# Matmuls that read hi first and lo last in every group, and rotations and rows of scales asked for later

## The chip, the cores and the metric

The kernel runs on one core of one Trainium2 chip. The metric is device time in microseconds (us) of one execution, lower is better. The kernel before takes 2664.11 us, the median of three runs (2663.95 to 2665.12).

## The reference

Two layers of an encoder on 256 tokens of width 2048, in float32. Cut to what matters:

```python
for l in range(DEPTH):                                  # DEPTH = 2
    u = rmsnorm(x, norm_mix[l])
    c_q, c_kv, k_pe, q_na, k_na, v_na, gate_a, gate_b = split(u @ w_in[l])
    q  = rmsnorm(c_q,  norm_qa[l])  @ w_uq[l]           # 8 heads of 128 + 64 (rotary)
    kv = rmsnorm(c_kv, norm_kva[l]) @ w_ukv[l]          # 8 heads of 128 + 128
    y_a = mla_attention(q_nope, rope(q_pe), k_nope, rope(k_pe), v) @ w_o_mla[l]
    y_b = neighbourhood_attention(q_na, k_na, v_na, rpb[l]) @ w_o_na[l]
    x = x + (sigmoid(gate_a) * y_a + sigmoid(gate_b) * y_b) @ w_out[l]
    h = rmsnorm(x, norm_mlp[l]) @ w_ff1[l]              # 2048 -> 8192
    x = x + square(relu(h)) @ w_ff2[l]                  # 8192 -> 2048
return rmsnorm(x, norm_final)
```

Nearly all of the arithmetic is products of 256 rows with weight matrices of 2048 or more rows and columns, some 490 MB of them read once.

## The kernel before, in words

**Split operands.** Every float32 operand of a product is split in two: `hi` is the value rounded to the matmul's input type `F32R`, `lo` is the rest. A product then is three matmuls into one PSUM bank: activation hi times weight hi, activation hi times weight lo, activation lo times weight hi. The product lo times lo is left out. Activations are split once. Weights are split as they arrive: a DMA on the SP queue brings `raw`, ScalarE (ACT) casts `hi <- raw` (line 177 or 201), and VectorE (DVE) subtracts `lo <- raw - hi` (line 178 or 202). `raw` has 3 buffers; `hi` and `lo` have 4 each in the first half of a layer and 3 each in the second half (`strips`), where a buffer holds 2048 columns instead of 1024.

**Forms of a product.**
- `gemm_a` (weights stream, activations stand; lines 232 to 234 through `mm_a`): two banks, one for each 128 tokens. A group is two k-blocks of 128 rows: for each of the two banks 2 x 3 matmuls of 512 columns, then one `tick()`.
- `gemm_b` (activations stream, weights stand; lines 223 and 224 through `mm_b`): four banks. A pair is one matmul of 512 columns with `wh`, which covers activation hi and lo at once, and one of 256 columns with `wl`. A group is 4 x 2 pairs with a `tick()` after every second pair.
- `gemm_s` (line 414 through `mm3`): 1024 columns of the weights at a time with up to eight banks. A step `j` takes 256 rows of the weights. A step that is not in `pairs` has 8 products of 3 matmuls (24). A step in `pairs` is a Strassen-like one with 7 products (21 matmuls): DVE forms four sums of the four weight blocks (lines 446, 449, 450) into `sums`, which ACT and DVE split in hi and lo as well. The first three products (1, 2, 3) read `raw`, the last four (5, 7, 6, 4) read `sums`. There are 110 such steps, one for each instruction of line 446. At the first step in `pairs`, `drain()` asks for all pending work at once.

**What else runs.** Smaller work (heads of the attention, norms, transposes, rotations) is written as generators on a list `pending`. `tick()` counts a clock and advances one generator whose time has come; `yield n` and `start(gen, n)` mean "not before n more ticks". So ticks, not times, place this work among the matmuls. `rows_of` turns a column of scales into a row (DVE builds `diag`, TensorE multiplies with ones on line 283). `rope` is a rotation: a TensorE product with a permutation (line 517), three DVE operations and a split. `turned` transposes a merged tile on TensorE (line 484) after DVE has written it (lines 782, 783). `evac` functions empty the banks when a product is done.

**Order.** The kernel is built with `tile.TileContext(nc, schedule_with_timeline_sim=True)`: the order in the source is a priority, and a planner with its own estimates of durations writes each engine's queue before the program runs. An engine takes its queue in that order.

Of the kernel before, what the change touches and what calls it, by code (L numbers as in the profile page):

```python
# [39 lines left out]
P = 128  # L40
S = 256
# [10 lines left out]
NC = D // P  # L52
# [23 lines left out]
def trunk(ctx: ExitStack, tc: tile.TileContext, x, w_in, w_uq, w_ukv, rpb, w_o_mla, w_o_na,  # L76
# [80 lines left out]
    def have(acts, k):  # L157

        while acts[k] is None:
            advance(min(range(len(pending)), key=lambda i: pending[i][0]))  # L160
        return acts[k]
# [59 lines left out]
    def mm_b(ps, wh, wl, a, first, last):  # L221

        nc.tensor.matmul(ps, wh, a, start=first, stop=False)  # L223
        nc.tensor.matmul(ps[:, :S], wl, a[:, :S], start=False, stop=last)  # L224

    def mm_a(ps, a, t, wh, wl, first, last):

        if isinstance(a, list):
            ah, al = a[0][t], a[1][t]
        else:  # L230
            ah, al = a[:, t * P:(t + 1) * P], a[:, S + t * P:S + (t + 1) * P]
        nc.tensor.matmul(ps, ah, wh, start=first, stop=False)  # L232
        nc.tensor.matmul(ps, ah, wl, start=False, stop=False)  # L233
        nc.tensor.matmul(ps, al, wh, start=False, stop=last)  # L234

    def mm_3(ps, ah, al, bh, bl, first, last):
# [11 lines left out]
    def gemm_a(w, c0, acts, evac):  # L248

        nk = len(acts)  # L250
        ps = [bank() for _ in range(2)]
        for k0, wh, wl in weights(w, nk, c0, 512):
            for t in range(2):
                for k in range(k0, k0 + 2):
                    mm_a(ps[t], have(acts, k), t, wh[:, k - k0], wl[:, k - k0], k == 0, k == nk - 1)
                tick()
        for t in range(2):
            evac(t, ps[t])

    def gemm_b(w, c0, acts, evac, before=None, ahead=None):  # L260

        nk = len(acts)
        ps = [bank() for _ in range(4)]
        for k0, wh, wl in weights(w, nk, c0, 512, before):
            for m in range(4):
                ms = slice(m * P, (m + 1) * P)
                for k in range(2):
                    mm_b(ps[m], wh[:, k, ms], wl[:, k, ms], have(acts, k0 + k), k0 + k == 0, k0 + k == nk - 1)
                tick()
        if ahead:  # L270
            ahead()
        for m in range(4):
            evac(m, ps[m])

    def rows_of(col):

        dg = [keep.tile([P, P], F32, tag="diag", name="diag", bufs=4) for _ in range(2)]
        for t in range(2):
            nc.vector.tensor_scalar_mul(dg[t], ident, col[:, t:t + 1])
        yield 5  # L280
        pb = abank()
        for t in range(2):
            nc.tensor.matmul(pb[:, t * P:(t + 1) * P], ones, dg[t], start=True, stop=True)
        row = keep.tile([P, S], F32, tag="rrow", name="rrow", bufs=4)
        nc.vector.tensor_copy(row, pb[:, :S])
        return row
# [113 lines left out]
    def gemm_s(w, c0, get, order, pairs, evac):  # L400
# [7 lines left out]

        def mm3(i, ah, al, wh, wl):
            if i not in b:  # L410
                b[i], count[i] = bank(), 0
            for x, y in ((ah, wh), (ah, wl), (al, wh)):
                count[i] += 1
                nc.tensor.matmul(b[i], x, y, start=count[i] == 1, stop=count[i] == total[i])  # L414

# [8 lines left out]
        for j in order:  # L424
# [3 lines left out]
            if j not in pairs:  # L428
                ws = cut(raw)
                for k in range(2):  # L430
                    left, right = ws[2 * k:2 * k + 2]
                    ah, al = get(j)
                    for i, t, side in ((2, 0, right), (3, 0, left), (4, 1, right), (8, 1, left)):
                        mm3(i, ah[2 * k + t], al[2 * k + t], *side)
                        if t:
                            tick()
                continue
# [15 lines left out]
            (a11, _, a12, a22, s1, s2, s3, s4), (l11, _, l12, l22, r1, r2, r3, r4) = get(j)  # L453
            mm3(1, a11, l11, *w11)
            mm3(2, a12, l12, *w21)
            tick()
            mm3(3, s4, r4, *w22)
            mm3(5, s1, r1, *w1)
            tick()
            mm3(7, s3, r3, *w3)  # L460
            mm3(6, s2, r2, *w2)
            tick()
            mm3(4, a22, l22, *w4)
        r11, r22, r12, r21 = (wide() for _ in range(4))
# [182 lines left out]
    for l in range(DEPTH):  # L647
# [15 lines left out]
        for g in range(2):  # L663
# [5 lines left out]
            for k0, wh, wl in weights(wi, NC, C_VN + g * 512, 512):  # L669
                for t in range(2):  # L670
                    for k in range(k0, k0 + 2):
                        mm_a(ps[t], xg[k], t, wh[:, k - k0], wl[:, k - k0], k == 0, k == NC - 1)
                    tick()
                    tick()
            vt = [values(ps[t], mix.col, t) for t in range(2)]
# [26 lines left out]
        nc.vector.tensor_tensor(t, t, mix.row, op=ALU.mult)  # L702
        start(rope(t, key_pe(ke)), 4)

# [28 lines left out]
        for g in range(4):  # L733
# [7 lines left out]
            nc.vector.tensor_tensor(t, t, nq.row, op=ALU.mult)  # L741
            start(rope(t, query_pe(qr)), 3)
            for m in range(2):
# [207 lines left out]
```

## Time and profile before

| what | us |
|---|---|
| median of three runs | 2664.11 |
| the profiled execution | 2664.57 |
| its span, first to last instruction | 2662.8 |
| TensorE matmul (PE) busy | 2616.6 (98%) |
| TensorE weight load (PEld) busy | 2181.1 (82%) |
| VectorE (DVE) busy | 2121.3 (80%) |
| ScalarE (ACT) busy | 1461.4 (55%) |

The mean granted TensorE clock is 0.999. DMA engines are busy 55% of the span with the weights' queue. A matmul's duration in the profile runs over the start of the next one, since they are pipelined: what a matmul takes from the others is the distance from its start to the next start. A row of the view of waits reads: who waited, for whom, microseconds in total, times, longest.

### The profile page before, as it was taken

The numbers are of one execution on the slowest core, as the hardware profiler recorded it, in microseconds if no ns is written. First come the engines' busy times: TensorE is split into PE (matmuls) and PEld (weight loads), VectorE is DVE, ScalarE is ACT, GpSimd is POOL, SyncE is SP. The second block draws the span as 40 slices with busy tenths as digits, with TensorE's granted clock in tenths as the row PEclk, the third lists the DMA queues.
The fourth block names the chain that finished last, engine by engine and source line by source line (L and its number), as shares of the span: only waits on it lengthen the run. The fifth ranks groups of instructions, "written<-read, shape, count | busy, mean of one in ns | idle before, by whom it ended". The sixth has DMA issues, their size and how long they took to land.

```text
span 2662.8 us, 31999 instructions
## 1 busy us (share of the span) xinstructions
PE 2616.6 (98%) x12498; PEld 2181.1 (82%) x12498; DVE 2121.3 (80%) x2496; ACT 1461.4 (55%) x1719; POOL 94.8 (4%) x117
## 2 busy tenths in 40 slices
PE   8999999999999999999999999999999999999998
PEld 7888888877888888888888888888788888888886
DVE  6678789688888787888667788896988888878885
ACT  6555456446555545546555555564565555455553
POOL 0100000000000010000001100000000000100000
PEclk9999999999999999999999999999999999999999
DMA  7555554455567485675555555544555765756744
GB/s 245 176 159 196 195 201 147 158 174 188 192 201 237 163 239 197 197 236 177 189 185 179 165 191 190 203 141 152 182 202 172 219 206 196 236 199 194 253 168 144
DMA packets 175256, 508.95 MB, mean 191 GB/s; under 512 B 13696, under 2 KB 18176, under 8 KB 175104
## 3 DMA queue, kind: packets, MB, share of 16 engines
q1 hardware_dynamic: 166192, 490.08, 55.2%
q0 software_dynamic: 8768, 16.78, 3.2%
q8 instruction: 98, 1.61, 0.2%
q14 instruction: 54, 0.44, 0.0%
q10 hardware_dynamic: 144, 0.04, 0.0%
HBM read 492.18 MB, written 2.10 MB: 186 GB/s over the span
## 4 chain that ended last, share of the span: by engine, by line
PE 68%; issue 21%; DVE 6%; ACT 3%; POOL 1%; DMA 0%; POOLq 0%; DVEq 0%; ACTq 0%; SPq 0%
PE bank L414 40%; PE bank L223 8%; PE bank L224 4%; PE bank L232 4%; PE bank L233 4%; PE bank L234 4%; DVE lo L178 3%; ACT hi L177 2%; PE bank L383 1%; PE bank L239 1%; PE bank L238 1%; PE bank L237 1%; DVE wide L465 1%; DVE sums L446 1%; POOL xt L862 1%
## 5 line engine op out<-in xcount | busy, mean ns | idle before, releaser
L414 PE MATMUL bank<-hi,pair 128*128 128x512 f32 x5156 | 1604.8, 391 | 9.8 <-ACT hi L177 9.1
L414 PEld LDWEIGHTS bank<-hi,pair 128*128 128x128 f32 x5156 | 965.6, 188 | 221.9 <-ACT hi L177 23.5
L414 PE MATMUL bank<-lo,pair 128*128 128x512 f32 x2578 | 1006.6, 391 | 7.7 <-DVE lo L178 7.7
L177 ACT CAST hi<-raw 128x2048 fp32r<-128x2048 f32 (+3 forms) x416 | 632.4, 1534 | 433.8 <-PE bank L414 302.4
L178 DVE TENSOR_TENSOR lo<-raw,hi 128x2048 fp32r<-128x2048 f32 (+3 forms) x416 | 752.0, 1817 | 117.6 <-ACT hi L177 115.9
L414 PEld LDWEIGHTS bank<-lo,pair 128*128 128x128 f32 x2578 | 483.9, 188 | 114.2 <-DVE lo L178 14.9
L178 DVE TENSOR_TENSOR lo<-sums,hi 128x2048 fp32r<-128x2048 f32 (+1 forms) x134 | 255.9, 1909 | 161.5 <-ACT hi L177 161.4
L202 DVE TENSOR_TENSOR lo<-raw,hi 128x1024 fp32r<-128x1024 f32 (+1 forms) x224 | 270.2, 1212 | 141.1 <-ACT hi L201 140.8
L177 ACT CAST hi<-sums 128x2048 fp32r<-128x2048 f32 (+1 forms) x134 | 214.8, 1603 | 286.1 <-DVE sums L450 185.0
L223 PE MATMUL bank<-pair,hi 128*128 128x512 f32 x960 | 344.5, 402 | 3.7 <-ACT hi L201 3.7
L201 ACT CAST hi<-raw 128x1024 fp32r<-128x1024 f32 (+1 forms) x224 | 229.9, 1035 | 205.2 <-PE bank L234 96.1
L224 PE MATMUL bank<-pair,lo 128*128 128x256 f32 x960 | 264.5, 281 | 0.0
L232 PE MATMUL bank<-hi,pair 128*128 128x512 f32 (+1 forms) x576 | 218.9, 381 | 0.0
L233 PE MATMUL bank<-lo,pair 128*128 128x512 f32 (+1 forms) x576 | 218.6, 380 | 0.0
L234 PE MATMUL bank<-hi,pair 128*128 128x512 f32 (+1 forms) x576 | 217.2, 378 | 0.0
L465 DVE TENSOR_TENSOR wide<-wide,bank 128x512 f32<-128x512 f32 x336 | 215.3, 678 | 0.1
L223 PEld LDWEIGHTS bank<-pair,hi 128*128 128x128 f32 x960 | 180.5, 189 | 42.2 <-ACT hi L201 4.5
L224 PEld LDWEIGHTS bank<-pair,lo 128*128 128x128 f32 x960 | 181.7, 189 | 2.3
L446 DVE TENSOR_TENSOR sums<-raw 128x1024 f32<-128x1024 f32 x110 | 134.1, 1219 | 21.9 <-DMA raw<-in_w_ff 14.5
L234 PEld LDWEIGHTS bank<-hi,pair 128*128 128x128 f32 x576 | 108.3, 188 | 19.9
L232 PEld LDWEIGHTS bank<-hi,pair 128*128 128x128 f32 x576 | 108.3, 188 | 20.0
L233 PEld LDWEIGHTS bank<-lo,pair 128*128 128x128 f32 x576 | 108.4, 188 | 18.9
(123 smaller groups left out, 1557.0 us busy)
## 6 DMA issues: line engine op xcount, KB each, us to landing
raw<-in_w_ff SPq DMA_DIRECT2D x256, 1024.0 KB, 5.3
raw<-in_w_in SPq DMA_DIRECT2D x124, 1024.0 KB, 5.1
raw<-in_w_out SPq DMA_DIRECT2D x32, 1024.0 KB, 5.3
raw<-in_w_o_na SPq DMA_DIRECT2D x16, 1024.0 KB, 5.1
raw<-in_w_o_mla SPq DMA_DIRECT2D x16, 1024.0 KB, 5.0
xt<-wide POOLq DMA_DIRECT2D x48, 256.0 KB, 7.3
raw<-in_w_ukv SPq DMA_DIRECT2D x8, 1024.0 KB, 5.5
raw<-in_w_uq SPq DMA_DIRECT2D x8, 768.0 KB, 4.6
```

Source lines behind the costliest of these rows:

```text
L177: nc.scalar.copy(hi, src)
L178: nc.vector.tensor_tensor(lo, src, hi.bitcast(F32), op=ALU.subtract)
L201: nc.scalar.copy(hi, src)
L202: nc.vector.tensor_tensor(lo, src, hi.bitcast(F32), op=ALU.subtract)
L223: nc.tensor.matmul(ps, wh, a, start=first, stop=False)
L224: nc.tensor.matmul(ps[:, :S], wl, a[:, :S], start=False, stop=last)
L232: nc.tensor.matmul(ps, ah, wh, start=first, stop=False)
L233: nc.tensor.matmul(ps, ah, wl, start=False, stop=False)
L234: nc.tensor.matmul(ps, al, wh, start=False, stop=last)
L414: nc.tensor.matmul(b[i], x, y, start=count[i] == 1, stop=count[i] == total[i])
L446: nc.vector.tensor_tensor(ts[0].rearrange("p (a n) -> p a n", a=2), raw[:, :512].rearrange("p (a n) -> p a n", a=1).to_broadcast([P, 2, 512]),
L465: add = lambda o, a, c: nc.vector.tensor_tensor(o, a, c, op=ALU.add)
```

## The change

Within each group of `gemm_a`, `gemm_b` and `gemm_s` all matmuls that read `hi` of the weights are asked for first and those that read `lo` last. In `gemm_s` a step's 7 or 8 products are now handed to `products`, which issues two matmuls of each with `wh`, with a tick after every second product, and then one of each with `wl`. `gemm_a` becomes `group_a`, with a third tick after the lo matmuls; the values' product of the neighbourhood attention, which had four ticks a group, uses it too with one more tick (four again). The products with `mm_b` and `mm_a` in the loops over `w_uq`, `w_ukv` and the key rotation's columns stay as they are. `rows_of` yields 8 ticks instead of 5; the key rotation is started 8 ticks after its input instead of 4, the query rotations 7 instead of 3. The number, shapes and operands of all matmuls are the same.

```diff
+    def group_a(ps, acts, k0, nk, wh, wl):
+        for t in range(2):
+            for k in range(2):
+                for i, a in enumerate(sides(have(acts, k0 + k), t)):
+                    nc.tensor.matmul(ps[t], a, wh[:, k], start=k0 + k + i == 0, stop=False)
+            tick()
+        for t in range(2):
+            for k in range(2):
+                nc.tensor.matmul(ps[t], sides(have(acts, k0 + k), t)[0], wl[:, k], start=False, stop=k0 + k == nk - 1)
+        tick()
...
 gemm_a:
-            for t in range(2):
-                for k in range(k0, k0 + 2):
-                    mm_a(ps[t], have(acts, k), t, wh[:, k - k0], wl[:, k - k0], k == 0, k == nk - 1)
-                tick()
+            group_a(ps, acts, k0, nk, wh, wl)
 gemm_b:
             for m in range(4):
                 for k in range(2):
-                    mm_b(ps[m], wh[:, k, ms], wl[:, k, ms], have(acts, k0 + k), ...)
+                    nc.tensor.matmul(ps[m], wh[:, k, m * P:(m + 1) * P], have(acts, k0 + k), ...)
                 tick()
+            for m in range(4):
+                for k in range(2):
+                    nc.tensor.matmul(ps[m][:, :S], wl[:, k, m * P:(m + 1) * P], have(acts, k0 + k)[:, :S], ...)
 rows_of:
-        yield 5
+        yield 8
 gemm_s:
+        def products(*todo):
+            for n, (i, ah, al, wh, wl) in enumerate(todo):
+                mm(i, ah, wh)
+                mm(i, al, wh)
+                if n % 2:
+                    tick()
+            for i, ah, al, wh, wl in todo:
+                mm(i, ah, wl)
...
-            mm3(1, a11, l11, *w11)
-            mm3(2, a12, l12, *w21)
-            tick()
-            mm3(3, s4, r4, *w22)
-            mm3(5, s1, r1, *w1)
-            tick()
-            mm3(7, s3, r3, *w3)
-            mm3(6, s2, r2, *w2)
-            tick()
-            mm3(4, a22, l22, *w4)
+            products((1, a11, l11, *w11), (2, a12, l12, *w21), (3, s4, r4, *w22), (5, s1, r1, *w1),
+                     (7, s3, r3, *w3), (6, s2, r2, *w2), (4, a22, l22, *w4))
...
-        start(rope(t, key_pe(ke)), 4)
+        start(rope(t, key_pe(ke)), 8)
...
-            start(rope(t, query_pe(qr)), 3)
+            start(rope(t, query_pe(qr)), 7)
```

More of the change, by code (lines that the diff above doesn't have):

```diff
@@ L224, in mm_b, with sides @@
         nc.tensor.matmul(ps[:, :S], wl, a[:, :S], start=False, stop=last)
+    def sides(a, t):
+        if isinstance(a, list):
+            return a[0][t], a[1][t]
+        return a[:, t * P:(t + 1) * P], a[:, S + t * P:S + (t + 1) * P]
     def mm_a(ps, a, t, wh, wl, first, last):
[L228 to L231, printed above, removed]
+        ah, al = sides(a, t)
         nc.tensor.matmul(ps, ah, wh, start=first, stop=False)
@@ L265, in gemm_b @@
             for m in range(4):
-                ms = slice(m * P, (m + 1) * P)
                 for k in range(2):
-                    mm_b(ps[m], wh[:, k, ms], wl[:, k, ms], have(acts, k0 + k), k0 + k == 0, k0 + k == nk - 1)
+                    nc.tensor.matmul(ps[m], wh[:, k, m * P:(m + 1) * P], have(acts, k0 + k), start=k0 + k == 0, stop=False)
                 tick()
+            for m in range(4):
+                for k in range(2):
+                    nc.tensor.matmul(ps[m][:, :S], wl[:, k, m * P:(m + 1) * P], have(acts, k0 + k)[:, :S],
+                                     start=False, stop=k0 + k == nk - 1)
         if ahead:
@@ L407, in gemm_s, with mm @@
                 total[i] += 3 if j in pairs else 6
-        def mm3(i, ah, al, wh, wl):
+        def mm(i, x, y):
             if i not in b:
                 b[i], count[i] = bank(), 0
-            for x, y in ((ah, wh), (ah, wl), (al, wh)):
-                count[i] += 1
-                nc.tensor.matmul(b[i], x, y, start=count[i] == 1, stop=count[i] == total[i])
+            count[i] += 1
+            nc.tensor.matmul(b[i], x, y, start=count[i] == 1, stop=count[i] == total[i])
+        def products(*todo):
[6 more added lines that the diff above has]
+                mm(i, ah, wl)
         def cut(src):
@@ L429, in gemm_s @@
                 ws = cut(raw)
[L430 to L435, printed above, removed]
-                            tick()
+                ah, al = get(j)
+                products(*((i, ah[2 * k + t], al[2 * k + t], *ws[2 * k + side])
+                           for k in range(2) for i, t, side in ((2, 0, 1), (3, 0, 0), (4, 1, 1), (8, 1, 0))))
                 continue
@@ L453, in gemm_s @@
             (a11, _, a12, a22, s1, s2, s3, s4), (l11, _, l12, l22, r1, r2, r3, r4) = get(j)
-            mm3(1, a11, l11, *w11)
-            mm3(2, a12, l12, *w21)
-            tick()
-            mm3(3, s4, r4, *w22)
-            mm3(5, s1, r1, *w1)
-            tick()
-            mm3(7, s3, r3, *w3)
-            mm3(6, s2, r2, *w2)
-            tick()
-            mm3(4, a22, l22, *w4)
+            products((1, a11, l11, *w11), (2, a12, l12, *w21), (3, s4, r4, *w22), (5, s1, r1, *w1),
+                     (7, s3, r3, *w3), (6, s2, r2, *w2), (4, a22, l22, *w4))
         r11, r22, r12, r21 = (wide() for _ in range(4))
@@ L669, in trunk @@
             for k0, wh, wl in weights(wi, NC, C_VN + g * 512, 512):
[L670 to L674, printed above, removed]
+                group_a(ps, xg, k0, NC, wh, wl)
+                tick()
             vt = [values(ps[t], mix.col, t) for t in range(2)]
```

## The prediction, made before the change was run

> **What bounds the kernel now.** I read the page's busy times first, then the view of waits, then the timeline at a few of those waits, then groups by shape.
>
> ```profile
> span 2662.8 us, 31999 instructions
> PE 2616.6 (98%) x12498; PEld 2181.1 (82%) x12498; DVE 2121.3 (80%) x2496; ACT 1461.4 (55%) x1719; POOL 94.8 (4%) x117
> ```
>
> TensorE is the bound: the same 12498 matmuls run after the change, so only the time that PE stands still, and the distance between two matmuls, can change. The view of waits says what it stands still for.
>
> ```profile
> PEld bank L414 <- ACT hi L177: 23.5, 34, 1.0
> PEld bank L414 <- DVE lo L178: 14.9, 22, 1.8
> PE bank L414 <- ACT hi L177: 9.1, 24, 0.5
> PE bank L414 <- DVE lo L178: 7.7, 11, 1.4
> PE bank L484 <- DMA xt<-in_x: 4.9, 1, 4.9
> PE bank L517 <- DVE small L741: 4.1, 4, 1.5
> PE bank L223 <- ACT hi L201: 3.7, 2, 2.5
> PE bank L484 <- DVE wide L783: 3.3, 4, 1.2
> PE bank L283 <- DVE diag L279: 1.0, 2, 0.5
> ACT hi L177 <- PE bank L414: 397.2, 231, 6.0
> DVE lo L178 <- ACT hi L177: 277.3, 209, 3.5
> ACT hi L177 <- DVE sums L450: 185.0, 41, 7.1
> ```
>
> PE's own rows hold 33.8 us, of which the waits for x and for line 201 are mostly the start. The last three rows are the loop behind the waits of line 414: ACT waits 231 times until PE has let go of a `hi` buffer, and DVE's `lo` follows ACT. How much one wait costs is seen in the timeline at 562 us:
>
> ```profile
> 562.50 0.19 PEld L414 LDWEIGHTS bank<-lo,pair 128*128 128x128 f32 x1 [1.85 <-DVE lo L178]
> 562.50 0.50 PE L414 MATMUL bank<-lo,pair 128*128 128x512 f32 x1 [1.43 <-DVE lo L178]
> 562.84 0.39 PE L414 MATMUL bank<-hi,pair 128*128 128x512 f32 x1
> 563.07 0.40 PE L414 MATMUL bank<-lo,pair 128*128 128x512 f32 x1
> ```
>
> Undisturbed matmuls start 0.23 us apart (562.84, 563.07), though each is shown as 0.39 long. So an idle time in PE's rows leaves out 0.39 - 0.23 = 0.16 us, and the first matmul after a wait takes 0.34 instead of 0.23 (562.50 to 562.84), 0.11 more. A wait in these rows costs its idle time and 0.27 us.
>
> **The change, part by part.**
>
> *Waits for lo (`gemm_s`).* Today the second matmul of a step reads lo, 0.23 us after the first. After, it comes behind all 14 or 16 hi matmuls, 3.2 to 3.7 us in. The longest wait for lo is 1.4 us on PE, 1.8 on PEld, so all go, if DVE is not slower. What is there: 7.7 + 11 x 0.27 = 10.7 us. By PEld's rows, whose loads start 0.23 apart and take 0.19, it would be at most 14.9 - 22 x 0.04 = 14.0. What hides lo afterwards are the hi matmuls; were hi late too, the gain would be nil. I take 10.7.
>
> *Waits for hi (`gemm_s`).* The order moves no hi matmul behind anything new, but its buffer is free sooner: today the last matmul of a step reads hi, after the change 7 or 8 lo matmuls stand behind the last one that does, 1.6 to 1.8 us. Whether the late cast was waiting for that buffer is seen at two places:
>
> ```profile
> 736.90 1.92 ACT L177 CAST hi<-raw 128x2048 fp32r<-128x2048 f32 x1 [2.70 <-PE bank L414]
> 739.23 1.48 ACT L177 CAST hi<-raw 128x1536 fp32r<-128x1536 f32 x1
> 740.77 0.50 PE L414 MATMUL bank<-hi,pair 128*128 128x512 f32 x1 [0.28 <-ACT hi L177]
> 569.23 3.29 ACT L177 CAST hi<-raw 128x2048 fp32r<-128x2048 f32 x2
> 569.66 1.07 PE L414 MATMUL bank<-hi,pair 128*128 128x512 f32 x4
> 571.19 0.97 PE L414 MATMUL bank<-hi,pair 128*128 128x512 f32 x3 [0.46 <-ACT hi L177]
> ```
>
> At 736.90 ACT had idled 2.70 us for the buffer, and the next cast, 1.48 long, came 0.28 late: 1.6 us earlier there removes it. At 569.23 two casts follow each other with no idle time, so ACT was late for another reason, and an earlier buffer alone doesn't help. There is a second help: at 569.66 PE had run ahead with four hi matmuls, because the planner thought lo late; with lo asked for last it has less reason to. Present: 9.1 + 24 x 0.27 = 15.6 us (at most 23.5 - 34 x 0.04 = 22.1 by PEld). Ends: all gone, or none. I take two thirds, 10.4, nearer to the first row, because 231 waits of ACT for the buffer speak for it.
>
> *Which stages.* The losses sit where DVE is fullest, around w_out and the first ff1, and at the start of each ff2:
>
> ```profile
> 545.00:625.00 80.00, 75.52 (x332) 60.57 (x333) 69.69 (x76) 42.57 (x47) 0.00 (x0) 1.00 0.57 185
> 733.00:763.00 30.00, 29.21 (x129) 23.14 (x127) 24.31 (x28) 19.02 (x19) 0.00 (x0) 1.00 0.51 172
> ```
>
> PE (first number after the length) lacks 4.5 of 80 us in the first, twice in the program, and 0.8 of 30 in the second, eight times. DVE (third) is busy 87% and 81%: there is room to catch up, not much.
>
> *Order in `gemm_b`.* 12 calls of 8 groups, each of 8 matmuls of 512 and 8 of 256 columns.
>
> ```profile
> 1503.22 0.40 PE L223 MATMUL bank<-pair,hi 128*128 128x512 f32 x1
> 1503.46 0.28 PE L224 MATMUL bank<-pair,lo 128*128 128x256 f32 x1
> ```
>
> The third such pair after it ends where the next 512 columns start; and near the start of the program the planner put some in a row:
>
> ```profile
> 1504.28 0.40 PE L223 MATMUL bank<-pair,hi 128*128 128x512 f32 x1
> ```
>
> ```profile
> 23.02 1.09 PE L223 MATMUL bank<-pair,hi 128*128 128x512 f32 x4
> 23.95 0.28 PE L224 MATMUL bank<-pair,lo 128*128 128x256 f32 x1
> 24.30 0.40 PE L224 MATMUL bank<-pair,lo 128*128 128x256 f32 x2
> ```
>
> In turn, three pairs take 1504.28 - 1503.22 = 1.06 us, 0.353 a pair. In a row, 512 columns follow each other at (1.09 - 0.40) / 3 = 0.230, 256 columns at 0.40 - 0.28 = 0.12. A group becomes 7 x 0.230 + 0.24 + 7 x 0.12 + 0.117 = 2.81 instead of 2.82: 0.01 to 0.02 less, for 96 groups 1 to 2 us; with the rounding of these rows between 0 and 5. I take 2. The Trainium skill, "TensorE: Matmul & The Clock Gate", section Back-to-back issue gap, gives the distance as columns over the clock and a small constant, 216 ns for 512 columns and 109 for 256 as an estimate from that page, whatever stands next to what; by that the order would be worth exactly nothing, and the sum 2 us less. The rows (230 and 120, and 240 in turn) disagree mildly, and they decide.
>
> *Rotations of the queries.* `rope` is asked for 4 ticks later; a tick there is two pairs, 0.7 us, so 2.8 us more cover than today, against waits of at most 1.5 us. Present: 4.1 + 4 x 0.16 = 4.7 us. If the planner had already put it where it thought DVE ready, it may move less than 2.8; ends 0 and 4.7, I take 4.5, since the four waits exceed their cover by less than what is added. The heads that read the rotated queries are queued after 12 ticks, so nothing waits in turn.
>
> *Rows of scales.* The two waits of line 283 (1.0 us) come after the `drain()` of the first gate product, which asks at once, whatever `yield` says: nil, at most 1.3.
>
> *Key rotation.* Eight ticks after its start that same drain comes, so the rotation's DVE work (three operations of 0.42 and two splits) now meets the first sums:
>
> ```profile
> 231.07 0.42 DVE L521 TENSOR_TENSOR small<-small 128x256 f32<-128x256 f32 x1
> ```
>
> Five of these are 2.1 us in front of the sums in each layer: between 0 and 4.2 us, I take 1 lost, since lo has its new slack there.
>
> *Merges before w_out.* `gemm_a` ticks three times a group instead of two, so `turned`, four ticks after a merge, is asked for after 16 matmuls instead of 24, 1.8 us sooner, while the bank it waits for is finished later (below). Line 484 already waits 3.3 + 4 x 0.16 = 3.9 us. Six merges could lose up to 1.8 each, 10.8; the planner may also put it right, 0. I take half of what is there, 2.0 lost.
>
> *Queues.* SP's loads wait for `raw`, which lo frees; lo comes no later, so they move sooner or not at all. POOL's loads of the bias keep their ticks.
>
> ```profile
> SPq L426 <- DVE lo L178: 1385.5, 271, 13.3
> ```
>
> *End.* The last `gemm_a` finishes its first bank 2 matmuls before its end instead of 6; 0.2 us later for the final norm.
>
> Sum against the profiled execution: 2664.6 - 10.7 - 10.4 - 2 - 4.5 + 1 + 2 + 0.2 = 2640.2. That execution is 0.5 above the median of the runs, so 2639.7, say **2640**.
>
> **The rivals.**
>
> *B, hi stays late.* Lo's waits go, hi's all stay: 2639.7 + 10.4 = 2650. For it: 569.23 above. Against it: the 231 waits for the buffer.
>
> *C, the change does not do what it says.* The planner already puts hi first wherever it expects lo late (569.66: four hi in a row, which the source never has more than two of). If it sees the same lateness in the new order, the waits of line 414 stay and only the rotations gain: 2664.1 - 4.5 + 3.2 = 2663. Against it: waits for lo are there today, so its expectations are off by more than nothing.
>
> *D, slower: hi of the sums is needed sooner.* In each of the 110 Strassen steps the sums' hi is read after 6 matmuls instead of 9, 0.69 us sooner, and DVE makes them:
>
> ```profile
> L177 ACT CAST hi<-sums 128x2048 fp32r<-128x2048 f32 x86 | 164.4, 1912 | 214.8 <-DVE sums L450 185.0 <-PE bank L414 29.1
> L178 DVE TENSOR_TENSOR lo<-sums,hi 128x2048 fp32r<-128x2048 f32 x86 | 197.1, 2292 | 130.3 <-ACT hi L177 130.2
> L178 DVE TENSOR_TENSOR lo<-raw,hi 128x1536 fp32r<-128x1536 f32 x86 | 150.7, 1752 | 15.0 <-ACT hi L177 14.9
> L446 DVE TENSOR_TENSOR sums<-raw 128x1024 f32<-128x1024 f32 x110 | 134.1, 1219 | 21.9 <-DMA raw<-in_w_ff 14.5 <-DMA raw<-in_w_in 6.8
> L450 DVE TENSOR_TENSOR sums<-raw,sums 128x512 f32<-128x512 f32 x110 | 75.4, 686 | 1.4
> ```
>
> A step costs DVE 1.22 + 2 x 0.69 + 1.75 + 2.29 = 6.6 us (line 449 as 450), against 21 x 0.23 = 4.8 on PE. If a step loses 0.69 + 0.11 = 0.80, 31 steps eat up the gain of 24.4; with half of the 110, 2640 + 44 = 2684. For it: ACT waits 185 us for line 450. Against it: PE waited for any cast only 24 times, most casts lie well ahead, and the sums' buffer is free 1.6 us sooner as well.
>
> *E, slower: banks finish together.* All four banks of a `gemm_b` now end within 8 x 0.12 us: the first is done 0.72 instead of 2.1 us ahead of the end, 1.4 later, 12 times; in `gemm_a` 0.45 instead of 1.36, 0.9 later, 24 times. Were PE to wait for each: 16.8 + 21.6 = 38 us, 2678. Today PE waits for an emptied bank in no row, only for the merges (line 783), and the next product takes other banks. The Trainium skill, "Perfetto Trace Analysis", section Optimizing Tensor Performance, asks for products that rotate through banks so that emptying one overlaps the next product; within a product the change does the opposite, which speaks against it, and by that rule this case would be likelier than the rows let me make it.
>
> **How the numbers follow.** A (2629 to 2648) 0.52, and better than that, with nearly all waits gone, 0.09; B (2648 to 2658) 0.17; C 0.10; D 0.07; E 0.05. Faster by over 0.2% (5.3 us, about what a measurement here can tell from no change) is A, the better case and B, 0.78; within it C, 0.10; slower 0.12. The low end takes all of PE's waits for hi and lo by PEld's bound with nothing lost: 2664 - 14 - 22 - 4.7 - 3 = 2620; the high end goes to C's near side, 2660. That leaves out D, E and most of C, 0.2.
>
> **What would show it.** In the view of waits the row of line 414 for lo should fall under 2 us, the one for hi to a third (3 us), the row of line 517 vanish, that of line 484 grow to 4 or 5; line 283 should stay. From 545 to 625 us PE should be busy some 78 of 80 us, and ACT's 397 us of waiting for PE should shrink. Two lo matmuls of `gemm_b` should start 0.12 apart. I am wrong if hi's row stays or grows (B, D), with the sums as its releaser for D, or if line 223, 232 or 414 waits for a bank's reader (E).

## The result and the profile after

| | us | ratio to before [95% interval] |
|---|---|---|
| before, median beside it on the same chip | 2664.19 (2663.95 to 2665.12) | |
| after, median | 2630.63 (2630.19 to 2630.92) | 0.9873 [0.9856, 0.9890] |
| after, the profiled execution | 2630.92, span 2629.1 | |

The change gains 33.6 us; the forecast was 24 (2640, range 2620 to 2660). One of the five runs of x7_hhl below took 11707.87 us, for a reason that no trace shows; without it x7's median is 2648.23 instead of 2648.31. The page's busy times after:

```profile
PE 2599.1 (99%) x12498; PEld 2183.3 (83%) x12498; DVE 2116.7 (81%) x2496; ACT 1457.8 (55%) x1719; POOL 97.2 (4%) x117
```

The matmuls are as many as before, and DVE and ACT are as busy as before within 5 us. Only PE's standing still has become less. The view of waits of after; the first eight rows are all that PE has:

```profile
PE bank L428 <- ACT hi L177: 6.2, 6, 1.1
PE bank L495 <- DMA xt<-in_x: 4.7, 1, 4.7
PE bank L279 <- ACT hi L201: 3.2, 1, 3.2
PE bank L279 <- DVE pair L168: 1.3, 1, 1.3
PE bank L252 <- DVE pair L168: 1.2, 2, 0.6
PE bank L428 <- ACT pair L407: 0.5, 2, 0.3
PE bank L252 <- ACT pp L560: 0.4, 2, 0.2
PE bank L495 <- ACT wide L501: 0.3, 1, 0.3
...
PEld bank L428 <- ACT hi L177: 9.9, 8, 1.6
...
ACT hi L177 <- PE bank L428: 424.2, 243, 7.5
DVE lo L178 <- PE bank L428: 84.4, 56, 3.6
```

Line 428 is the old 414, 279 the old 223, 495 the old 484, 528 the old 517, 298 the old 283. PE's rows hold 17.8 us in 16 waits against 33.8 in 48. With 0.27 us beside each wait that is 16.0 + 32 x 0.27 = 24.6 of the 33.6 us. PEld's waits on that line that were too short to show on PE went from 21 (34 + 22 less 24 + 11) to 2 (8 less 6). No row of PE's has lo as its releaser any more, and DVE now waits 84 us for lo's own buffer, which stays in use to the end of a step.

The two stretches whose losses the prediction showed, by the same windows:

```profile
545.00:625.00 80.00, 79.03 (x356) 65.05 (x355) 74.68 (x76) 48.48 (x50) 0.00 (x0) 1.00 0.64 207
733.00:763.00 30.00, 30.00 (x134) 24.86 (x133) 25.18 (x25) 16.25 (x12) 0.97 (x1) 1.00 0.63 206
```

PE went from 75.52 to 79.03 of 80 us and from 29.21 to 30.00 of 30. The fixed windows lie a little further on in the program than before, since everything runs earlier, so they don't tell the whole gain of a stage. The lead does: the start of the k-th matmul in before less that in after. It is 2.1 us where w_out starts in layer 1 (539 us in before) and 8.5 in the first ff1 (657 us); in layer 2 it goes over the same stages from 20.8 (1861 us) to 25.6 (1978 us). At each of the eight starts of an ff2 it grows by 1.4 to 2.0 us, 13.6 together. So some 25 of the 33.6 us are gained in the stages that the prediction named.

The starts also divide the whole gain among the lines, roughly, since a distance between two matmuls depends on both. The matmuls of `gemm_s` take 22.9 us less, the rotations' 5.9, the transposes of merged tiles 4.4, those of `gemm_b`'s form 2.7 and the rows of scales 1.6; the rest, above all the attention heads' products and transposes, takes 3.9 more.

What is left of line 428's waits for hi is three places in each layer, 1.14 + 1.13 + 0.82 us, twice. Timeline rows of after, at the start of the first gate product, at the start of w_out and inside w_out:

```profile
230.95 0.61 PE L428 MATMUL bank<-hi,pair 128*128 128x512 f32 x2
231.60 1.04 ACT L177 CAST hi<-raw 128x1024 fp32r<-128x1024 f32 x1 [3.21 <-DVE small L531]
232.70 0.96 PE L428 MATMUL bank<-hi,pair 128*128 128x512 f32 x3 [1.14 <-ACT hi L177]
...
539.40 3.93 PE L428 MATMUL bank<-hi,pair 128*128 128x512 f32 x16 [1.13 <-ACT hi L177]
...
561.89 1.91 ACT L177 CAST hi<-sums 128x2048 fp32r<-128x2048 f32 x1 [0.95 <-DVE sums L469]
562.19 0.62 PE L428 MATMUL bank<-hi,pair 128*128 128x512 f32 x2
562.64 0.39 PE L428 MATMUL bank<-lo,pair 128*128 128x512 f32 x1
563.86 2.53 PE L428 MATMUL bank<-hi,pair 128*128 128x512 f32 x8 [0.82 <-ACT hi L177]
```

The transposes of merged tiles (line 495) no longer wait for DVE in any row. At 563.86 PE needs hi of the sums, and ACT had itself stood 0.95 us for the last of the sums from DVE. That is the mechanism of rival D, once in a layer.

### The profile page after: what moved, and what is told of

The parts are those of the page before. It is cut to its first block, busy times and chain, and to the rows that moved or that the text cites. A ratio compares the mean times of both kernels' runs of the same rounds, so it can differ in the third digit from the quotient of the medians.

```text
span 2629.1 us, 32272 instructions
## 1 busy us (share of the span) xinstructions
PE 2599.1 (99%) x12498; PEld 2183.3 (83%) x12498; DVE 2116.7 (81%) x2496; ACT 1457.8 (55%) x1719; POOL 97.2 (4%) x117
## 4 chain that ended last, share of the span: by engine, by line
PE 76%; issue 19%; DVE 2%; ACT 1%; POOL 1%; DMA 0%; SPq 0%; POOLq 0%; DVEq 0%; ACTq 0%
PE bank L428 47%; PE bank L244 8%; PE bank L279 7%; PE bank L248 4%; PE bank L283 3%; PE bank L223 1%; PE bank L398 1%; DVE lo L178 1%; PE bank L252 1%; PE bank L224 1%; PE bank L254 1%; PE bank L253 1%; POOL xt L870 1%; PE bank L558 0%; ACT hi L177 0%
## 5 line engine op out<-in xcount | busy, mean ns | idle before, releaser
L428 PE MATMUL bank<-hi,pair 128*128 128x512 f32 x5156 | 1269.8, 390 | 7.0 <-ACT hi L177 6.2
L428 PEld LDWEIGHTS bank<-hi,pair 128*128 128x128 f32 x5156 | 964.9, 188 | 210.6 <-ACT hi L177 9.9
L428 PE MATMUL bank<-lo,pair 128*128 128x512 f32 x2578 | 677.4, 389 | 0.0
L428 PEld LDWEIGHTS bank<-lo,pair 128*128 128x128 f32 x2578 | 483.7, 188 | 100.2
L244 PE MATMUL bank<-hi,pair 128*128 128x512 f32 x1024 | 259.6, 390 | 0.0
L244 PEld LDWEIGHTS bank<-hi,pair 128*128 128x128 f32 x1024 | 190.6, 188 | 38.9
L279 PE MATMUL bank<-pair,hi 128*128 128x512 f32 x768 | 203.2, 397 | 4.5 <-ACT hi L201 3.2
L279 PEld LDWEIGHTS bank<-pair,hi 128*128 128x128 f32 x768 | 136.3, 190 | 26.9 <-ACT hi L201 3.6
L248 PE MATMUL bank<-lo,pair 128*128 128x512 f32 x512 | 142.8, 392 | 0.0
L283 PEld LDWEIGHTS bank<-pair,lo 128*128 128x128 f32 x768 | 106.9, 190 | 8.7
L283 PE MATMUL bank<-pair,lo 128*128 128x256 f32 x768 | 111.6, 283 | 0.0
L248 PEld LDWEIGHTS bank<-lo,pair 128*128 128x128 f32 x512 | 95.2, 188 | 18.9
L408 DVE TENSOR_TENSOR pair<-wide,pair 128x512 fp32r<-128x512 f32 x108 | 72.4, 686 | 13.9 <-ACT pair L407 13.9
L870 POOL DMA_DIRECT2D xt<-wide x48 | 42.3, 968 | 977.0 <-DVE wide L476 702.6
```

What stands on the lines that cost most here:

```text
L244: nc.tensor.matmul(ps[t], a, wh[:, k], start=k0 + k + i == 0, stop=False)
L248: nc.tensor.matmul(ps[t], sides(have(acts, k0 + k), t)[0], wl[:, k], start=False, stop=k0 + k == nk - 1)
L279: nc.tensor.matmul(ps[m], wh[:, k, m * P:(m + 1) * P], have(acts, k0 + k), start=k0 + k == 0, stop=False)
L283: nc.tensor.matmul(ps[m][:, :S], wl[:, k, m * P:(m + 1) * P], have(acts, k0 + k)[:, :S], start=False, stop=k0 + k == nk - 1)
L408: nc.vector.tensor_tensor(lw, src, h.bitcast(F32), op=ALU.subtract)
```

## The experiments

Each is compared with the kernel before on its own chip. The gain is the median's distance from the median of before there, whose own medians lie between 2664.2 and 2665.5. Kernels x start from before or after as their diffs say; y and z start from after.

| run | what it is | median | ratio [interval] | gain, us |
|---|---|---|---|---|
| after | all | 2630.63 | 0.9873 [0.9856, 0.9890] | 33.6 |
| x1_strassen | `gemm_s` alone | 2645.26 | 0.9926 [0.9912, 0.9939] | 19.6 |
| x2_plain | `gemm_a`, `gemm_b`, values | 2666.29 | 1.0004 [0.9996, 1.0013] | -1.4 |
| x3_lags | the later lags alone | 2669.88 | 1.0014 [1.0005, 1.0023] | -5.0 |
| x4_order | order everywhere, old lags | 2631.87 | 0.9875 [0.9862, 0.9889] | 33.0 |
| x7_hhl | before, lo last in each product | 2648.31 | 0.9935 [0.9921, 0.9948] | 17.2 |
| x5_hold_hi | after, two hi matmuls a step behind lo | 2651.32 | 0.9946 [0.9932, 0.9959] | 14.2 |
| y4_hold_half_b | the same, second half of a layer | 2642.10 | 0.9916 [0.9903, 0.9930] | 23.0 |
| x6_lo_mid | after, lo second of three passes | 2660.03 | 0.9980 [0.9971, 0.9989] | 5.5 |
| y1_gemm_a_old | after, `gemm_a` as before | 2645.67 | 0.9929 [0.9916, 0.9941] | 19.5 |
| y2_two_ticks | after, no third tick | 2635.37 | 0.9889 [0.9874, 0.9904] | 29.8 |
| y3_key_later | after, key rotation later | 2630.76 | 0.9872 [0.9859, 0.9886] | 34.4 |
| z1_raw_then_sums | after, Strassen step in two halves | 2630.60 | 0.9871 [0.9854, 0.9887] | 34.5 |

### One part at a time: x1, x2, x3, x4

**x1_strassen** is before with `products` in `gemm_s`, nothing else.

```diff
-            for x, y in ((ah, wh), (ah, wl), (al, wh)):
...
+            for n, (i, ah, al, wh, wl) in enumerate(todo):
+                mm(i, ah, wh)
+                mm(i, al, wh)
...
+            for i, ah, al, wh, wl in todo:
+                mm(i, ah, wl)
```

> Only gemm_s has hi first and lo last; gemm_a, gemm_b and all lags are as before. Theory 1 (the waits of the 44 gemm_s calls carry the gain): PE's waits for hi and lo on the line of gemm_s fall from 16.8 us to some 6, lo's row is gone, and the time is 2640 to 2645. Theory 3 (the gain is in the plain products): 2658 to 2664, the waits hardly changed.

Rows of its view of waits:

```profile
PE bank L413 <- ACT hi L177: 9.6, 8, 2.0
...
PE bank L413 <- DVE lo L178: 1.7, 2, 0.8
```

It gains 19.6 us, 58% of the whole, at the edge of what was expected. The profile is of the fastest of its five runs (2642.80). Waits for hi and lo are 11.3 us where some 6 were expected: those for lo fell from 7.7 us in 11 to 1.7 in 2. Those for hi became fewer, 24 to 8, but not smaller in sum (9.1 to 9.6): a few long ones of up to 2.0 us. Line 513 is the rotations', with their old lag; its row fell as well, from 4.1 to 2.4.

**x2_plain** is before with `group_a`, the new `gemm_b` and the values' product.

```diff
-                    mm_a(ps[t], have(acts, k), t, wh[:, k - k0], wl[:, k - k0], k == 0, k == nk - 1)
...
+            group_a(ps, acts, k0, nk, wh, wl)
...
-                    mm_b(ps[m], wh[:, k, ms], wl[:, k, ms], have(acts, k0 + k), k0 + k == 0, k0 + k == nk - 1)
```

> Only gemm_a, gemm_b and the values' product have hi first and lo last (with gemm_a's third tick); gemm_s and all lags are as before. Theory 1: 96 groups of gemm_b a little closer together (0 to 5 us less), the merges' wait up to 2 us more: 2659 to 2664. Theory 3: 2640 to 2645.

```profile
PE bank L532 <- DVE small L753: 5.6, 7, 1.5
...
PE bank L298 <- DVE diag L294: 3.0, 2, 1.5
PE bank L499 <- DVE wide L795: 1.9, 2, 1.0
```

It gains nothing that can be told. The row of merges (499) and that of lo (to 5.3 in 8) shrink by 1.4 and 2.4 us, while rotations (532), rows of scales (298) and hi (to 10.5 in 26) grow by 1.5, 2.0 and 1.4.

**x3_lags** is before with the three numbers alone.

```diff
-        yield 5
+        yield 8
...
-        start(rope(t, key_pe(ke)), 4)
+        start(rope(t, key_pe(ke)), 8)
...
-            start(rope(t, query_pe(qr)), 3)
+            start(rope(t, query_pe(qr)), 7)
```

> Only the three lags are changed (8, 8 and 7 ticks). Theory 1: the four waits for the query rotations go (4.7 us), the key rotation costs up to 1: 2659.5 to 2661. Rival: the planner had placed the rotations where it believes them ready, and the lag does nothing: 2664, with the waits of the rotation's line still there.

A row of its view of waits, where the row of line 517 is gone:

```profile
PE bank L484 <- DVE wide L783: 7.2, 4, 2.6
```

What I expected of it did not come: by the medians it is slower, by 1.4 parts in a thousand [0.5, 2.3], 3.7 us by that ratio and 5.0 by the medians. The 4.1 us of the rotations are gone, and 3.9 us stand instead at the merges before w_out (3.3 to 7.2): the wait moved on to the next user of DVE. It also became longer, up to 2.6 us in one piece, and something follows it that no row of waits shows. Rows of the timeline, and of the view of windows, whose third number from the end is the granted clock:

```profile
516.14 0.49 PE L484 MATMUL bank<-ident,wide 128*128 128x128 f32 x2 [2.59 <-DVE wide L783]
...
517.72 0.63 PE L232 MATMUL bank<-hi,pair 128*128 128x512 f32 x1
518.14 0.63 PE L233 MATMUL bank<-lo,pair 128*128 128x512 f32 x1
516.34:519.75 3.41, 3.41 (x10) 2.73 (x9) 3.41 (x5) 0.00 (x0) 0.00 (x0) 0.50 0.04 11
```

For 3.4 us the granted clock is one half, and matmuls of 512 columns start 0.43 us apart instead of 0.23: some 1.6 us lost. x3's trace has three such stretches, at 516.3, 1840.7 and 1871.4 us, 4.8 of the 6.1 us by which its span exceeds that of before (2668.9 against 2662.8). The traces of before and after have none until their last 11 us. The runs without a trace agree: of x3's eleven, the six with a granted clock of 0.996 took 2669.88 to 2670.69 us, the four with 0.998 took 2664.99 to 2667.84, against 2663.63 to 2666.91 for before on that chip. So the later lags by themselves cost little, 1.3 us by this trace; what makes x3 slower is mostly the half clock.

In the kept traces there are twelve of these stretches ahead of the end of a kernel: three here, two each in x2, x5, x6 and y1, one in z1. Each begins within 1.3 us, before or after, of the end of a wait of PE of 0.9 us or more. Not every such wait has one: x1 has two of 2.0 us and after has one of 3.2 us at its start, with none. That the longer waits bring on the half clock fits all twelve, but no run tests it.

**x4_order** is after with the three old lags (the x3 diff, backwards).

> The changed order everywhere, with the old lags (5, 4 and 3). Theory 1 (parts add up): 2634 to 2635, the waits for the query rotations back with 4 to 5 us. Rival (in the new order the rotations find other cover): 2630 to 2632.

```profile
PE bank L528 <- DVE small L749: 2.4, 6, 0.8
```

It gains 33.0 of the 33.6 us. In the new order the rotations' row is 2.4 us and the lags that remove it are worth 0.6 by the gains, 1.2 by the medians: less than this measurement can tell from nothing.

So the parts don't add up: 19.6 - 1.4 - 5.0 = 13.2, and together 33.6. In x1 and x2 each half of the order leaves the other half's waits. By the medians about 15 us (33.0 - 19.6 + 1.4) exist only where both are there. By the traces' spans, with the half clock of x2 (two stretches, some 3 us) put aside, it is some 10: x4 gains 32.4, x1 21.8 and x2 about 0.5.

### Which half of the new order in `gemm_s` counts: x7, x6, x5, y4

Lo later (cover for DVE) and hi's buffer free sooner (cover for ACT) come together in the change. x5, y4 and x6 hold hi back and keep lo late; x7 moves both, by one matmul in the source.

**x7_hhl** is before with the order hi, hi, lo inside each product: lo moves by one matmul, and so does hi's last reader.

```diff
-            for x, y in ((ah, wh), (ah, wl), (al, wh)):
+            for x, y in ((ah, wh), (al, wh), (ah, wl)):
```

> The kernel before, with one thing changed: within each product of gemm_s the order is hi, hi, lo instead of hi, lo, hi. lo is needed one matmul (0.23 us) later and hi comes free one matmul sooner. If lateness counts by its length (both theories): a small part of it, 2658 to 2663. If it only counts that the planner has a hi matmul to put in front: half of the gain or more, under 2650.

```profile
PE bank L414 <- ACT hi L177: 3.3, 8, 0.6
PE bank L414 <- DVE lo L178: 3.0, 4, 0.9
PE bank L484 <- DVE wide L783: 1.4, 4, 0.4
```

One swap in one line gains 17.2 us, nearly what x1 gains: the second of the two cases expected. 24 hi waits became 8, 11 lo waits 4, and the merges' row fell from 3.3 to 1.4. It is tempting to say that a shift of one matmul, 0.23 us, does much against waits of 9.1 / 24 = 0.38 us, but the shift in PE's queue is not of one matmul:

```profile
571.72 2.43 PE L414 MATMUL bank<-hi,pair 128*128 128x512 f32 x10
573.99 1.07 PE L414 MATMUL bank<-lo,pair 128*128 128x512 f32 x4
```

In the trace of before, the 2578 lo matmuls of line 414 stand one by one between hi ones, with a single pair, and at most eight hi follow each other. In x7 there are 276 groups of three to five lo, and up to fourteen hi follow each other. With lo last in each product the planner can put more hi ahead of a lo that it thinks late, and it did. What a shift of 0.23 us alone would gain, no run shows.

**x5_hold_hi** is after, with two of a step's matmuls that read hi put behind the lo ones, so that lo stays late and hi's buffers are freed at the step's end. In a Strassen step of the second half of a layer these are the last readers of both hi tiles, in the first half of two of its four.

```diff
+            held = (2, 6) if len(todo) == 7 else (3, 7)
             for n, (i, ah, al, wh, wl) in enumerate(todo):
                 mm(i, ah, wh)
-                mm(i, al, wh)
+                if n not in held:
+                    mm(i, al, wh)
...
+            for n in held:
+                i, ah, al, wh, wl = todo[n]
+                mm(i, al, wh)
```

> The changed kernel, but in gemm_s the last matmul that reads each hi tile (of products 3 and 7 of a Strassen step, 4 and 8 of another) stands behind the lo matmuls: lo is asked for as late as in the changed kernel, and a hi buffer comes free only at the end of the step, as in the kernel before. Theory 1 (the earlier free hi buffer carries the hi part of the gain): PE's waits for hi come back, 8 to 11 us, 2638 to 2642. Theory 2 (lo asked for late carries all of it, because the planner then doesn't run ahead): 2629 to 2633.

```profile
PE bank L428 <- ACT hi L177: 7.6, 14, 0.9
PE bank L298 <- DVE diag L294: 6.7, 2, 3.3
```

It loses 19.4 of the 33.6 us. The row of line 298, which after does not have, is part of that: 6.7 + 2 x 0.27 = 7.2 us stand at the rows of scales at the first gate product, ahead of w_out and ff. At the end of each of these two waits the granted clock is one half, for 3.4 us (from 235.1) and 6.8 us (from 1545.9), some 4 us more. Hence the next one.

**y4_hold_half_b** holds hi in the second half of a layer only.

```diff
+            held = () if not strips else (2, 6) if len(todo) == 7 else (3, 7)
```

> The changed kernel with the last hi matmuls held behind the lo matmuls as in the run before that did so, but only in w_out, ff1 and ff2; the gate products keep the changed order, so the long wait for the rows of scales there has no cause. Theory 1 (a hi buffer that comes free late costs about half of the gain of these stages, 4 us a layer in the ff blocks and 2 to 4 around w_out): 2640 to 2646. Theory 2 (only lo's lateness counts, and the loss of the run before was all in the gate products): 2630 to 2634.

```profile
PE bank L428 <- ACT hi L177: 9.8, 14, 1.1
```

The row of line 298 is gone, and 10.6 us (23.0 against 33.6) are still lost. In the ff blocks of layer 1 the view of waits by PEld, from 660 to 1275 us, has no row at all for after; for y4 it has this one and two small ones (0.5 us for lo, 0.3 for an activation):

```profile
PEld bank L428 <- ACT hi L177: 4.0, 9, 1.3
```

One of y4's late casts, just ahead of that stretch, with the wait that it causes:

```profile
655.71 1.91 ACT L177 CAST hi<-sums 128x2048 fp32r<-128x2048 f32 x1 [4.54 <-PE bank L428]
657.67 1.25 PE L428 MATMUL bank<-hi,pair 128*128 128x512 f32 x3 [0.86 <-ACT hi L177]
```

ACT stood 4.54 us until PE had let go of a hi buffer, and PE then stood 0.86 us for that cast. y4's trace has no stretch of half clock but its end. So the early release of hi's buffer counts by itself: this is shown.

**x6_lo_mid** has three passes: activation hi times hi, then lo, then activation lo times hi.

```diff
                 mm(i, ah, wh)
-                mm(i, al, wh)
...
                 mm(i, ah, wl)
+            for i, ah, al, wh, wl in todo:
+                mm(i, al, wh)
```

> The changed kernel, but in gemm_s the lo matmuls stand in the middle of a step: first activation hi times weight hi of all products, then the lo matmuls, then activation lo times weight hi. lo is needed 7 or 8 matmuls (1.6 to 1.8 us) into the step, and hi buffers come free at its end. Theory 1: waits for lo mostly gone (the longest were 1.4 us), waits for hi back: 2638 to 2644. Theory 2: half of the lateness is enough for lo, hi follows: 2631 to 2635.

```profile
PE bank L428 <- ACT hi L177: 10.6, 27, 0.8
PE bank L298 <- DVE diag L294: 8.0, 2, 4.0
```

It keeps 5.5 us of the gain, less than I had allowed. Lo waits are nearly gone (2.2 us in 2), hi waits are those of before (9.1, 24), and 8.0 us stand at the rows of scales, with 3.4 us of half clock behind each of these two waits, another 3 us. Against x7 this says that covering lo while holding hi gives little: the two belong together.

### The part that the prediction had as a loss: y1, y2

**y1_gemm_a_old** is after, with `gemm_a` in its old order and its two ticks; `gemm_b`, the values, `gemm_s` and the lags stay new.

```diff
-            group_a(ps, acts, k0, nk, wh, wl)
+            for t in range(2):
+                for k in range(k0, k0 + 2):
+                    mm_a(ps[t], have(acts, k), t, wh[:, k - k0], wl[:, k - k0], k == 0, k == nk - 1)
+                tick()
```

> The changed kernel, but gemm_a has its old order and its two ticks a group. The order everywhere gave 33 us, gemm_s alone 20, the plain products alone nothing: 13 us exist only together. Theory 1 (they come from gemm_a just before w_out: its hi buffers come free earlier and the merges are asked for at other times, so w_out starts with less backlog): 2638 to 2644. Rival (they come from gemm_b, whose order only helps once gemm_s no longer makes up for it): 2631 to 2634.

The waits of its PE from 500 to 548 us, where the merges and the first weights of w_out meet:

```profile
PE bank L498 <- DVE wide L794: 2.6, 1, 2.6
PE bank L431 <- ACT hi L177: 2.0, 1, 2.0
```

After has one wait in that window, the 1.1 us at 539.40. 14.1 us are lost, and y1 is no faster than x1: without `gemm_a`'s change those of `gemm_b` and of the lags give nothing either. Some 3 of the 14 us are half clock, 3.4 us right at the end of each of the two 2.6 us waits for merges (from 516.2 and 1826.9 us).

**y2_two_ticks** is after, with `gemm_a` in its new order and two ticks.

```diff
                 nc.tensor.matmul(ps[t], sides(have(acts, k0 + k), t)[0], wl[:, k], start=False, stop=k0 + k == nk - 1)
-        tick()
```

> The changed kernel, but gemm_a ticks twice a group as before, with hi still first. If the third tick carries gemm_a's part (work between the matmuls is asked for sooner): the same as without gemm_a's change, 2638 to 2644. If the order carries it: 2630 to 2633. By the prediction's step on the merges the third tick costs 2 us: 2628 to 2629.

In its view of waits the merges have a row again, 1.4 us in each layer:

```profile
PE bank L494 <- DVE wide L791: 2.8, 2, 1.4
```

y2 is 4.6 us slower than y3, which ran on the same chip and equals after (2634.91 to 2636.17 against 2630.19 to 2631.38). So of the 14 us of `gemm_a` the tick is some 4 and the order some 10. What the tick does is seen in the transposes of the attention's heads, which sit among `gemm_a`'s matmuls; a line's instructions from 400 to 560 us, for before, after and y2:

```profile
L547 PE MATMUL bank<-ident,p x32: 270/272/273, 432.8 to 499.0; 128*128 128x128 f32 x32
```

```profile
L558 PE MATMUL bank<-ident,p x32: 270/272/273, 432.0 to 490.1; 128*128 128x128 f32 x32
```

```profile
L557 PE MATMUL bank<-ident,p x32: 270/272/273, 432.3 to 499.3; 128*128 128x128 f32 x32
```

With three ticks the last head is through at 490.1, 9 us sooner. That DVE then meets the merges with less in hand is the reading that fits; no run took it apart from the rest. The 10 us of the order can be read in y1 against y2: the rows of merges, of hi and of line 282 (y2's 278) for hi are 2.4, 1.6 and 1.6 us larger, and y1 has the some 3 us of half clock, y2 none. Why the old order of `gemm_a` makes DVE late at the merges, no run shows.

### Two attempts at what is left: y3, z1

**y3_key_later** starts the key rotation after the first gate product, to see whether it holds up the cast at 231.60.

```diff
-        start(rope(t, key_pe(ke)), 8)
...
         gemm_s(wi, C_GB, mixed, ORDER, MIXED, gate(part, 0))
+        start(rope(t, key_pe(ke)), 8)
```

> The changed kernel, but the key rotation is started after the first gate product instead of ahead of it, so that the drain no longer puts its splits in front of the first sums. Theory (ACT stands 3.2 us for the rotation's last DVE operation with the sums' cast behind it, and PE then 1.1 us for that cast, once a layer): 2 to 3 us less, 2627.5 to 2629. Rival (the cast is late for the sums anyway, or the wait moves to the rows of scales): 2630 to 2632.

The time is that of after, and the wait of 1.1 us is still there. The key rotation costs nothing there. The profile of after names line 531, DVE's rotation work, as the releaser of the cast at 231.60; with that work moved the wait stayed, so the name was not the cause. The cause is in y3's timeline:

```profile
229.32 0.62 PE L428 MATMUL bank<-hi,pair 128*128 128x512 f32 x2
229.97 1.04 ACT L177 CAST hi<-raw 128x1024 fp32r<-128x1024 f32 x1 [2.80 <-PE bank L428]
```

The cast waits for a hi buffer, and starts 0.03 us after the last two hi matmuls end (229.94). In after the same two matmuls end at 231.56, 0.04 us ahead of the cast, while line 531 happened to end at 231.58. So in y3, and by the same sign in after, PE still waits for hi at this place because hi's buffer comes free late.

**z1_raw_then_sums** cuts a Strassen step into its three products on `raw` (hi, then lo) and its four on `sums`, so that the sums' hi is asked for three matmuls later, as it was in before.

```diff
-            products((1, a11, l11, *w11), (2, a12, l12, *w21), (3, s4, r4, *w22), (5, s1, r1, *w1),
-                     (7, s3, r3, *w3), (6, s2, r2, *w2), (4, a22, l22, *w4))
+            products((1, a11, l11, *w11), (2, a12, l12, *w21), (3, s4, r4, *w22))
+            products((5, s1, r1, *w1), (7, s3, r3, *w3), (6, s2, r2, *w2), (4, a22, l22, *w4))
```

> The changed kernel, but a Strassen step of gemm_s runs its two halves one after the other: hi then lo of the three products that read raw, then hi then lo of the four that read sums. The sums' hi is then needed after 9 matmuls again instead of 6, lo of raw after 6 instead of 14, and the buffer of raw's hi comes free 8 matmuls sooner, that of the sums' hi as before. Theory (what is left of hi's waits is the sums' hi, asked for 0.68 us too soon, as at 563.86 us, 0.82 us once a layer): 1 to 2 us less than the changed kernel, 2628.5 to 2630. Rival (lo's lateness in the Strassen steps is what counts): waits for lo come back, 2633 to 2640.

The timeline of z1 at the place that is 563.86 in after:

```profile
563.60 0.62 PE L428 MATMUL bank<-hi,pair 128*128 128x512 f32 x2
564.05 0.39 PE L428 MATMUL bank<-lo,pair 128*128 128x512 f32 x1
565.26 1.66 PE L428 MATMUL bank<-hi,pair 128*128 128x512 f32 x6 [0.82 <-ACT hi L177]
```

Nothing changed, in time or in the wait. PE's queue at that place was the same already: in after too four hi, three lo, two hi and one lo matmul stand ahead of the wait (the last two rows of both are shown). The planner had pulled the lo matmuls ahead of a hi that it thought late. On the whole line 428 the order of hi and lo differs between the two traces at 248 of 7734 places. None of these versions beats after.

## Why the prediction was right or wrong, step by step

**The bound and the sign: right.** PE is the bound, and the gain is waits of PE. Rival C (the planner sees the same lateness) is refuted by x1 and x7, B and E by the rows: hi's row fell, and no product of the weights waits for a bank's reader. (The one such row of PE's, 0.3 us for line 501, is at the transposes of x at the program's start.) The Trainium skill, "Perfetto Trace Analysis", section Optimizing Tensor Performance, asks that the emptying of one bank overlap the next group; in this trace banks of a `gemm_b` finish together and PE waits for none, so the wait that this rotation is meant to prevent did not arise here.

**Waits for lo, 10.7: right.** The row is gone, and x1 alone brings it to 1.7. With hi's part the forecast for `gemm_s` was 21.1 us; by the starts its matmuls take 22.9 less.

**Waits for hi, 10.4 of 15.6: present, but by half a reason.** What is left is 6.2 + 6 x 0.27 = 7.8, so 7.8 went. That the buffer's release counts is shown by y4 (10.6 us). But my evidence for it was weak: ACT's waiting for PE, which "should shrink", grew from 397.2 in 231 to 424.2 in 243, and in y4, with more waits for hi, it is smaller (416.3 in 219). The row adds up the few casts that come late because of the buffer and the many that wait for it and are early all the same, so its size says neither. And x7 takes two thirds of the hi waits away with hi's last reader only one matmul sooner in the source, in part at least by another way, more hi matmuls ahead of a lo. The three places left are the starts of two products and the sums; at the first of them it is still the buffer (y3).

**Order in `gemm_b`, 2: right.** A group of after, in its timeline:

```profile
1500.41 2.00 PE L279 MATMUL bank<-pair,hi 128*128 128x512 f32 x8
1502.25 1.12 PE L283 MATMUL bank<-pair,lo 128*128 128x256 f32 x8
1503.20 2.00 PE L279 MATMUL bank<-pair,hi 128*128 128x512 f32 x8
```

1503.20 - 1500.41 = 2.79 us against the 2.82 of before: 0.03 x 96 = 2.9 us at most. By the Trainium skill's rule ("TensorE: Matmul & The Clock Gate", Back-to-back issue gap) the order would have been worth zero; in these rows it is worth about one part in a hundred of a group.

**Rotations, 4.5: mis-sized.** The row vanished as forecast, but a wait's row is not the price of removing it (and I had priced these waits at 0.16 us beside the idle time, the others at 0.27, without a reason). Alone the lags gained nothing (x3), because the wait moved on to the merges and became longer there; in the new order they were worth 0.6 to 1.2 (x4), because the order had already cut the row to 2.4. I asked what cover they get and not who uses DVE next.

**Rows of scales, 0: right in time, wrong in the row.** The row of line 283 went, though I had said it would stay; at its place stands a wait for hi of 1.14. Its sensitivity I missed: 3.0 in x2, 6.7 in x5, 8.0 in x6.

**Key rotation, +1: nothing** (y3).

**Merges before w_out, +2.0: the step that failed, in sign.** Line 484's row was to grow to 4 or 5; it vanished. I counted that `turned` is asked for 1.8 us sooner and its bank finished later, and forgot that a tick advances every pending generator: the heads ahead of the merges end 9 us sooner as well. y2 puts the tick at some 4 us gained, y1 the whole of `gemm_a` at 14, some 3 of it half clock, of which my sum had none.

**Rival D: its mechanism exists at one place in each layer**, 0.82 us, not at 31 of the 110 steps; the planner puts lo ahead of a late hi (z1).

**The total.** 24.4 forecast, 33.6 measured. With the terms as measured it is 24.4 - 4 (rotations) - 2.6 (hi) + 1 (key rotation) + 2 + 14 (`gemm_a`, for its loss forecast) = 34.8, which closes as well as parts that depend on each other can. Of the 33.6 us, 24.6 are counted in PE's waits and at most 2.9 in `gemm_b`'s spacing. The rest, about 6, are delays too short for these rows: the starts put 22.9 us at `gemm_s` where the rows of hi and lo give 7.8 + 10.7 = 18.5, and of the distances between matmuls of 512 columns those that are 0.06 to 0.12 us above 0.23 fell from 138 to 91. That the total came within 9 us owes something to luck: the merges' loss that did not come and the gain of `gemm_a` that was not in the sum stand on one side, rotations and hi that gave less than forecast on the other.

## What to carry to other kernels

Where one operand of a product arrives in two parts one after the other, order each group so that the part that arrives last is read last and the part whose buffer is wanted first is let go first; try the smallest swap first, since one line (x7) gave half of the gain here, and then compare the queues, not the sources, since the planner made more of that swap than one place. A large sum of a producer's waits for buffers says neither slack nor trouble by itself; look at the casts for which the reader waited. Don't price one part by its row of waits: the parts here sum to 13 us alone and gave 33.6 together, since a wait that is removed is taken up by the next user of the same engine until that one has cover too. And look at the longest wait, not only at the sum: in x3, x5, x6 and y1, at the end of waits of 2.6 to 4.0 us in the middle of the program, the granted clock fell to one half for 3.4 us or longer.

## What the runs showed that I had not expected

Moving small work later (x3) only moved its waits, into one longer wait with a stretch of half clock behind it, and moving the heads' work to end 9 us sooner gained. The releaser named in a row can be wrong: with line 531's work moved away PE waited as long as before for the cast at the gate's start, since the cast waits for a buffer (y3). And a swap of two words in the source can regroup an engine's queue (x7), while a larger reordering can leave it nearly as it was (z1), so a run without an effect says something of the mechanism only after its timeline has been compared.
